# A two-layer hybrid decoder on one core: a temporary in another buffer, the removal rate ahead of the receptance, and recurrence and query steps that follow no weight split

## The chip, the cores and the metric

One core of a Trainium2 chip runs the whole kernel in one launch. The metric is the device time of one execution in microseconds. In the profile PE is TensorE (matmuls), PEld its weight loads, DVE is VectorE, ACT is ScalarE, POOL is GpSimd, and SP is SyncE, which here only issues transfers. All data are float32.

## The reference, cut to what matters

Two layers on `x` of 1 x 256 x 2048. Each layer makes one wide input projection, feeds three mixers with its column groups, and ends in an output projection with a layer norm:

```python
for l in range(DEPTH):                       # 2 layers
    u = x @ w_in[l]
    (cb, cc, ch, cg, cq, ckv, kpe, mg, rcols, rg) = _split(u, IN_SIZES)
    y_conv = _short_conv_branch(cb, cc, ch, cg, conv_w[l])                # 512 columns
    y_mla = _mla_branch(cq, ckv, kpe, mg, ..., w_uq[l], w_ukv[l], cos, sin)  # 8 heads, 1024 columns
    y_rwkv = _rwkv7_branch(rcols, rg, ...)                                # 8 heads x 64
    mix = jnp.concatenate([y_conv, y_mla, y_rwkv], axis=-1)
    x = _layer_norm(DEEPNORM_ALPHA * x + mix @ w_out[l], ln_g[l], ln_b[l])
```

The RWKV mixer takes from `rcols` a receptance r, a key k, a value v, a decay w and a removal rate a (the last two by small two-step projections, `tanh(wd) @ w2` and `ad @ a2`), and runs this recurrence over the 256 positions:

```python
def step(state, inp):
    r_t, w_t, k_t, v_t, a_t, b_t = inp       # a = -kk, b = kk * a
    sa = jnp.einsum('bhvk,bhk->bhv', state, a_t)
    state = (state * w_t[:, :, None, :] + sa[..., None] * b_t[:, :, None, :]
             + v_t[..., None] * k_t[:, :, None, :])
    return state, jnp.einsum('bhvk,bhk->bhv', state, r_t)
```

## The kernel before

**Projections.** The input projection of a layer is cut into groups of 512 columns, named by what they give: `k`, `r`, `a` (removal rate and decay inputs with the attention's key and value inputs), `v`, `cq`, the convolution's `cc`, `ch`, `cb`, `cg`, and the gates `rg`, `mg0`, `mg1`. The list `MAIN` sets the order of the first ten. Then come the attention's second projections `ukv` and `uq`, then `mg0` and `mg1`, then the output projection `po`. A product is made from split operands: each float32 factor is a high part plus a low part, and `mm3` issues three matmuls for one (lines L338, L339, L340: high x high, high x low, low x high). A group is 16 row blocks of the weight x 4 column blocks x 3 = 192 matmuls, each 128x128 against 128x256.

**Weights.** SP loads a group's weight in four pieces of 1 MB (tiles `w_<group>`, three buffers). Each piece is split twice: ACT casts the high part (`hi_<group>`), DVE subtracts it for the low part (`lo_<group>`). There are four buffers of each, and one buffer pair feeds 24 matmuls.

**The mixers.** The branch code is written as generators (`rwkv`, `latent` for the attention, `conv`). For every weight split that PE consumes, `tick()` advances each running generator to its next `yield`; `until(name)` lets a generator wait until a group's matmuls are issued. A scheduler lays out every engine's order ahead of time by a simulated time line; steps issued under `tc.high_priority(AHEAD)` or `(EVICT)` go ahead of others. Each engine then runs its own list in that order, with semaphores where one waits for another.

**The gate.** `V` and `A` wrap VectorE and ScalarE. With `GATE = 'V'`, every VectorE step issued through `V` inside a tick is ordered behind the weight split two ahead of the one in use (`OFF = 2`). It is an order only, no semaphore. A step issued with `nc.vector` directly has no such bond, and `gates.clear()` takes it from the rest of a tick. `A` carries none in this setting.

**RWKV, step by step.** `rwkv_k` takes the key (`kx`, and its norm by `ksq`, `rn`, `kkn`). `rwkv_r` takes the receptance (`rx`). `rwkv_decay` mixes the decay and removal inputs (`wax`), splits them (`wah` on ACT, `wal` on DVE) and projects them with the split weight `was` in 16 matmuls (`pw`, `pa`; L528 and L529), then `sig`, `cum` and `pe`. `rwkv_products` makes the chunk products (`pg`, `gs`, from `ar` and `bk`), and SP carries them through DRAM in eight transfers `bd<-gs`. `rwkv_inverse` solves a triangular system by 31 steps on DVE, each with the temporary `tm` in pool `sm`, which has two buffers for a tag. `rwkv_pairs` transposes the keys and others (`pk`, L709). `rwkv_chain` is the recurrence over four chunks of 64 positions: PE `prh` (L782), DVE `rhs`, PE `pu` (L789), DVE and ACT `uvt`, PE `pst`, DVE `st`, which is the next chunk's state; after every second chunk PE makes the outputs `py` (L758, L767). `rwkv_norm` and `rwkv_gate` (`th_rg`) follow. These matmuls are small and use a half of the array's rows.

**Attention.** `mla_kv` makes keys and values (`pkn`, `pvt`), `mla_q` the queries (`pqn`, `pqp`), and `mla_attend` splits queries (`split_queries` into tiles `qk`, and `q1`) and runs the softmax over the heads.

PSUM has two pools of four buffers each: one for the accumulators of groups, one for everything else.

Of the kernel before, what the change touches and what calls it, by code (L numbers as in the profile page):

```python
# [10 lines left out]
F32 = mybir.dt.float32  # L11
# [3 lines left out]
ALU = mybir.AluOpType  # L15
AX = mybir.AxisListType

P = 128
D = 2048
S = 256  # L20
# [4 lines left out]
AHEAD = 1500  # L25
EVICT = 4000
# [84 lines left out]
def hybrid_layers(ctx: ExitStack, tc: tile.TileContext, x, positions, xT, w_in, w_out, w_uq, w_ukv, par, wa_in, gb_in,  # L111
                  gbp, cst, eye32, sums, out):
    nc = tc.nc
# [8 lines left out]
    sm = ctx.enter_context(tc.tile_pool(name="sm", bufs=2))  # L122
    dr = ctx.enter_context(tc.tile_pool(name="dr", bufs=1, space=bass.MemoryType.DRAM))

    gates, splits = {}, []
# [18 lines left out]
    V, A, G, T = Gated(nc.vector, "V"), Gated(nc.scalar, "A"), nc.gpsimd, nc.tensor  # L144
# [151 lines left out]
    def until(name):  # L296
        while name not in done:
            yield
# [46 lines left out]
        for i, src in enumerate((hi, lo)):  # L345
            T.matmul(o, ones[:, which * P:which * P + P], src, start=i == 0, stop=i == 1)

    MAIN, LATE, ORDER = ("k", "r", "a", "v", "cq", "cc", "ch", "cb", "cg", "rg"), ("mg0", "mg1"), (0, 12, 4, 8)

    def plan():  # L350

# [84 lines left out]
    def rwkv(l, pq, u, t):  # L436
        yield from until(f"k{l}")
        yield from rwkv_k(l, pq, t, u["k"][0])
        yield from until(f"r{l}")
        yield from rwkv_r(l, pq, t, u["r"][0])  # L440
        yield from until(f"a{l}")
        yield from rwkv_decay(l, pq, t, u["a"][0][0])
        yield from rwkv_scale(l, pq, t)
        yield from rwkv_products(l, t)
        inv = rwkv_inverse(l, t)
        while f"v{l}" not in done:
            next(inv)
            yield
        yield from rwkv_v(l, pq, t, u["v"][0])
        fill = rwkv_pairs(l, t)  # L450
        while True:
            a, b = next(inv, "end"), next(fill, "end")
            if a == b == "end":
                break
            yield
        yield from rwkv_chain(l, t)
        done.add(f"chain{l}")
        yield from rwkv_norm(l, pq, t)
        yield from until(f"heads{l}")
        yield from rwkv_gate(l, t)  # L460
# [166 lines left out]
    def rwkv_inverse(l, st):  # L627
        gs = st["gs"]
        bd = dr.tile([64, 32, 32], F32, tag=f"bd{l}", name=f"bd{l}")
        for par in range(2):  # L630
            for k in range(2):
                r = slice(par * 64 + k * 32, par * 64 + k * 32 + 32)
                u0 = (par * 2 + k) * 16
                for i in range(2):
                    src = gs[i].rearrange("p c (b q) t -> p c b q t", q=2)[r, :, :, par, k * 32:k * 32 + 32]
                    nc.sync.dma_start(bd[u0 + 8 * i:u0 + 8 * i + 8].rearrange("(c b) i j -> i c b j", b=4), src)
        bt = s4(f"bt{l}", (64, 32, 32))
        nc.sync.dma_start(bt, bd)
        xi = s4(f"xi{l}", (64, 32, 32))
        after(nc.sync.dma_start(xi, eye32.rearrange("p (i j) -> p i j", j=32)), st["mark"])  # L640
        yield
        yield
        yield
        n = 0
        for j in range(31, 0, -1):
            w = 32 - j
            tm = sm.tile([64, j, w], F32, tag="rt", name=f"tm{l}_{j}")
            V.tensor_tensor(tm, bt[:, 0:j, j:j + 1].to_broadcast([64, j, w]),
                            xi[:, j:j + 1, j:32].to_broadcast([64, j, w]), ALU.mult)
            V.tensor_tensor(xi[:, 0:j, j:32], xi[:, 0:j, j:32], tm, ALU.add)  # L650
            n += 1
            if n == 3:
                yield
                n = 0
        xd = dr.tile([64, 32, 32], F32, tag=f"xd{l}", name=f"xd{l}")
        nc.sync.dma_start(xd, xi)
        xq = s4(f"xq{l}", (P, 4, 4, 64))
        xt1 = sm.tile([P, 4, 4, 32], F32, tag="s", name=f"xt1{l}")
        V.memset(xq, 0.0)
        yield  # L660
        for par in range(2):
            for k in range(2):
                r = slice(par * 64 + k * 32, par * 64 + k * 32 + 32)
                u0 = (par * 2 + k) * 16
                nc.sync.dma_start(xq[r, :, :, k * 32:k * 32 + 32],
                                    xd[u0:u0 + 16].rearrange("(c b) i j -> i c b j", b=4))
        yield
        yield
        for par in range(2):
            r = slice(par * 64, par * 64 + 32)  # L670
            t1 = V.transpose(xt1[r].rearrange("p c b t -> p (c b) t"), xq[r, :, :, 0:32].rearrange("p c b t -> p (c b) t"))
        yield
        zs = sm.tile([P, 16, 32], F32, tag="s", name=f"zs{l}")
        quarters = [(slice(par * 64, par * 64 + 32), slice(par * 64 + 32, par * 64 + 64)) for par in range(2)]
        pz = [pm.tile([P, 16, 32], F32, tag="m", name=f"pz{l}_{par}") for par in range(2)]
        for c in range(4):
            for b in range(4):
                for par, (ra, rb) in enumerate(quarters):
                    m = T.matmul(pz[par][rb, c * 4 + b, :], gs[c // 2][ra, c % 2, 2 * b + par, 32:64],
                                 xt1[ra, c, b, :], start=True, stop=True)  # L680
                    if c == b == par == 0:
                        gather(m, [t1])
        for par, (ra, rb) in enumerate(quarters):
            z1 = V.tensor_copy(zs[rb], pz[par][rb])
        yield
        px = [pm.tile([P, 16, 32], F32, tag="m", name=f"px{l}_{par}") for par in range(2)]
        for c in range(4):
            for b in range(4):
                for par, (ra, rb) in enumerate(quarters):
                    m = T.matmul(px[par][ra, c * 4 + b, :], zs[rb, c * 4 + b, :], xq[rb, c, b, 32:64],  # L690
                                 start=True, stop=True)
                    if c == b == par == 0:
                        gather(m, [z1])
        for par, (ra, rb) in enumerate(quarters):
            st["xq1"] = V.tensor_copy(xq[ra, :, :, 32:64].rearrange("p c b t -> p (c b) t"), px[par][ra])
        yield
        st["xq"] = xq
# [47 lines left out]
    def rwkv_chain(l, st):  # L745
# [28 lines left out]
        for c in range(4):  # L774
            cc = slice(c * 64, (c + 1) * 64)
            if state is None:
                rhs = qs[:, 0]
            else:
                pr_ = pm.tile([P, 4, 64], F32, tag="m", name=f"prh{l}_{c}")
                for b in range(4):  # L780
                    for par in range(2):
                        T.matmul(pr_[rs[par], b, :], ar[rs[par], b, 0, cc], state[rs[par], b, :], start=True, stop=True)  # L782
                rhs = slot("rhs", f"rhs{l}_{c}", (P, 4, 64), 2)
                V.tensor_tensor(rhs, pr_, qs[:, c], ALU.add)
                yield
            pu = pm.tile([P, 4, 64], F32, tag="m", name=f"pu{l}_{c}")
            for b in range(4):
                for par in (1, 0):
# [3 lines left out]
            moved = []  # L792
            for par in range(2):
                dst = uvt[:, c].rearrange("p (b q) t -> p b q t", q=2)[rs[par], :, par, :]
                if par == 0:
                    moved.append(V.tensor_copy(dst, pu[rs[par]]))
                else:
                    moved.append(A.copy(dst, pu[rs[par]]))
            yield
            if c < 3:  # L800
                pst = pm.tile([P, 4, 64], F32, tag="m", name=f"pst{l}_{c}")
                for b in range(4):
                    for par in (1, 0):
                        h = 2 * b + par
                        m = T.matmul(pst[rs[par], b, :], bkt[:, c, h, :], uvt[:, c, h, :], start=True, stop=True)
                        if b == 0 and par:
                            gather(m, moved)
                new = slot("st", f"st{l}_{c}", (P, 4, 64), 2)
                pc_ = pe[:, c::4, 64:65].to_broadcast([P, 4, 64])
                if state is None:  # L810
                    V.tensor_tensor(new, pst, pc_, ALU.mult)
                else:
                    V.tensor_tensor(new, pst, state, ALU.add)
                    V.tensor_tensor(new, new, pc_, ALU.mult)
            before.append(state)
            if c % 2:
                out(c // 2, before[-2:], moved)
# [199 lines left out]
    def mla_attend(l, st):  # L1017
# [4 lines left out]
        def split_queries(h):  # L1022
            t = qk[h % 2]
            split_in(t[:, 0, 0:P], t[:, 1, 0:P], qn[:, h, P:S])
# [3 lines left out]
            split_queries(h)  # L1028
            split_keys(st, h)

        split_queries(0)
        for par in range(2):
            r, o = halves[par], halves[1 - par]
            of = lambda rr: q1.rearrange("p (g q) t -> p q g t", q=2)[rr, par]
            A.copy(of(r), qp[r, :, P:S])
            V.tensor_tensor(of(o), qp[r, :, P:S], of(r).bitcast(F32), ALU.subtract)
        split_queries(1)
        yield
        live = {}
        both = ((0, slice(0, 128)), (1, slice(128, 384)))  # L1040

# [362 lines left out]
```

## Time and profile before

| what | value |
|---|---|
| median of three runs | 920.2 us (920.05 to 921.54) |
| profiled execution, own time | 919.2 us |
| its span | 917.4 us |
| instructions | 18371 |
| mean granted TensorE clock | 0.996 of full speed |
| ACT busy | 467.1 us, 51% |
| POOL busy | 22.2 us, 2% |
| moved by DMA | 165.12 MB, mean 180 GB/s |

The span is what the hardware profiler saw of one execution; that execution's own time has 1.8 us around it. A profile row of a timeline gives the start in us, the duration in us, the engine, the line, the operation, output<-inputs with buffer numbers left out, sizes, and in brackets the idle time just before and what ended it. A helper records most steps of DVE and ACT, so these all carry line L137 and are told apart by tile names. The ends of matmuls are modelled; their starts are what to compare.

### The profile page before, as it was taken

Reading aid. Unit: us, or ns where it says so; the run is one execution under the profiler, and the core shown is the slowest. Engines: PE = TensorE matmul, PEld = TensorE weight load, DVE = VectorE, ACT = ScalarE, POOL = GpSimd, SP = SyncE. Lnnn points to the kernel's source line nnn. Section 1 sums busy time; section 2 is a strip of 40 time slices with the busy share of each in tenths; the row PEclk is TensorE's granted clock in tenths of the full one; section 3 lists DMA queues with packets and bytes.
Section 4 is the critical chain, followed back from the end, with each engine's and each line's share of the span. In section 5 each row is a group of like instructions: output and inputs, shape, how many; then the busy total and the mean of one; then the engine's idle time right before and its main releaser. Section 6 shows DMA issues by size and latency. Waiting matters only on the chain.

```text
span 917.4 us, 18371 instructions
## 1 busy us (share of the span) xinstructions
PE 905.3 (99%) x7719; PEld 865.5 (94%) x7719; DVE 670.8 (73%) x1122; ACT 467.1 (51%) x716; POOL 22.2 (2%) x47
## 2 busy tenths in 40 slices
PE   8999999999999999999999999999999999999996
PEld 8999999999999999888899999999999999998895
DVE  6686887885659986666766679878855599866665
ACT  6756546343447576434246474563424566764430
POOL 1210000000000000000010000000000000000000
PEclk9999999999999999999999999999999999999998
DMA  8955463455343643955565545545552456259442
GB/s 312 295 187 184 139 202 134 161 185 177 123 150 128 229 139 124 362 205 162 201 212 184 184 149 185 162 139 185 186 160 93 151 172 216 107 178 348 172 131 91
DMA packets 47523, 165.12 MB, mean 180 GB/s; under 512 B 13446, under 2 KB 22198, under 8 KB 32582
## 3 DMA queue, kind: packets, MB, share of 16 engines
q1 hardware_dynamic: 39680, 150.35, 47.9%
q10 hardware_dynamic: 5072, 9.57, 3.2%
q0 software_dynamic: 2688, 4.03, 1.6%
q8 instruction: 60, 0.98, 0.4%
q14 instruction: 23, 0.19, 0.1%
HBM read 158.61 MB, written 5.32 MB: 179 GB/s over the span
## 4 chain that ended last, share of the span: by engine, by line
PE 95%; DVE 2%; DMA 2%; ACT 0%; SPq 0%; issue 0%; DVEq 0%; ACTq 0%
PE po L338 6%; PE po L340 6%; PE po L339 6%; PE u_mg L340 3%; PE u_mg L338 3%; PE u_mg L339 3%; PE u_cc L338 2%; PE u_cg L340 2%; PE u_rg L340 2%; PE u_cq L340 2%; PE u_rg L338 2%; PE u_cg L338 2%; PE u_cb L340 2%; PE u_cb L339 2%; PE u_cb L338 2%; PE u_ch L339 2%
## 5 line engine op out<-in xcount | busy, mean ns | idle before, releaser
L137 DVE TENSOR_TENSOR lo_wo<-w_wo,hi_wo 128x1024 fp32r<-128x1024 f32 x57 | 69.3, 1222 | 45.9 <-ACT hi_wo L137 44.5
L137 ACT CAST hi_wo<-w_wo 128x1024 fp32r<-128x1024 f32 x57 | 59.7, 1052 | 72.9 <-PE po L340 61.5
L339 PE MATMUL u_mg<-x,hi_mg 128*128 128x256 f32 x256 | 72.7, 284 | 0.0
L340 PE MATMUL u_mg<-x,lo_mg 128*128 128x256 f32 x256 | 72.5, 283 | 0.0
L338 PE MATMUL u_mg<-x,hi_mg 128*128 128x256 f32 x256 | 72.1, 283 | 0.0
L340 PEld LDWEIGHTS u_mg<-x,lo_mg 128*128 128x128 f32 x256 | 49.1, 192 | 0.0
L339 PEld LDWEIGHTS u_mg<-x,hi_mg 128*128 128x128 f32 x256 | 49.0, 192 | 0.0
L338 PEld LDWEIGHTS u_mg<-x,hi_mg 128*128 128x128 f32 x256 | 48.9, 192 | 0.0
L339 PE MATMUL po<-lo_wo,ma 128*128 128x512 f32 (+1 forms) x128 | 46.4, 362 | 0.0
L340 PE MATMUL po<-hi_wo,ma 128*128 128x512 f32 (+1 forms) x128 | 46.4, 362 | 0.0
L338 PE MATMUL po<-hi_wo,ma 128*128 128x512 f32 (+1 forms) x128 | 45.9, 363 | 0.0
L137 DVE TENSOR_TENSOR lo_mg<-w_mg,hi_mg 128x1024 fp32r<-128x1024 f32 x32 | 38.9, 1221 | 7.2 <-ACT hi_mg L137 7.0
L137 ACT CAST hi_mg<-w_mg 128x1024 fp32r<-128x1024 f32 x32 | 33.5, 1048 | 17.0 <-PE u_mg L339 11.4
L338 PE MATMUL u_cc<-x,hi_cc 128*128 128x256 f32 x128 | 37.2, 290 | 0.0
L340 PE MATMUL u_cg<-x,lo_cg 128*128 128x256 f32 x128 | 37.0, 289 | 0.0
L340 PE MATMUL u_rg<-x,lo_rg 128*128 128x256 f32 x128 | 37.0, 289 | 0.0
L338 PE MATMUL u_rg<-x,hi_rg 128*128 128x256 f32 x128 | 36.8, 288 | 0.0
L338 PE MATMUL u_k<-x,hi_k 128*128 128x256 f32 x128 | 36.2, 287 | 0.4 <-ACT hi_k L137 0.4
L338 PE MATMUL u_cg<-x,hi_cg 128*128 128x256 f32 x128 | 36.4, 284 | 0.0
L339 PE MATMUL u_k<-x,hi_k 128*128 128x256 f32 x128 | 36.2, 286 | 0.0
L338 PE MATMUL u_a<-x,hi_a 128*128 128x256 f32 x128 | 36.2, 283 | 0.0
L339 PE MATMUL u_a<-x,hi_a 128*128 128x256 f32 x128 | 36.2, 283 | 0.0
(421 smaller groups left out, 3375.7 us busy)
## 6 DMA issues: line engine op xcount, KB each, us to landing
w_wo<-in_w_out_dram SPq DMA_DIRECT2D x24, 1024.0 KB, 5.2
w_mg<-in_w_in_dram SPq DMA_DIRECT2D x16, 1024.0 KB, 4.8
w_r<-in_w_in_dram SPq DMA_DIRECT2D x8, 1024.0 KB, 6.1
w_a<-in_w_in_dram SPq DMA_DIRECT2D x8, 1024.0 KB, 4.8
w_v<-in_w_in_dram SPq DMA_DIRECT2D x8, 1024.0 KB, 4.9
w_cq<-in_w_in_dram SPq DMA_DIRECT2D x8, 1024.0 KB, 4.9
w_cc<-in_w_in_dram SPq DMA_DIRECT2D x8, 1024.0 KB, 4.9
w_ch<-in_w_in_dram SPq DMA_DIRECT2D x8, 1024.0 KB, 4.9
```

The costliest lines, as they stand in the source:

```text
L137: inst = call(*args, **kwargs)
L338: m = T.matmul(o, lh, rh, start=first, stop=False, skip_group_check=True)
L339: T.matmul(o, lh, rl, start=False, stop=False, skip_group_check=True)
L340: T.matmul(o, ll, rh, start=False, stop=last, skip_group_check=True)
```

## The change

Four edits. (1) The inverse's temporary `tm` takes its buffers from tag "s" of the same pool instead of tag "rt". (2) Group `a` is projected ahead of group `r`, and `rwkv` runs the decay ahead of the receptance. (3) In the recurrence `rhs`, `uvt` and `st` on VectorE are issued with `nc.vector` under `high_priority(EVICT)`, so that the gate does not hold them, and the `yield` after `rhs` is gone. (4) `mla_attend` clears the gate and issues the query splits and `q1` at high priority, in another order, without a `yield` behind them.

```diff
-    MAIN, LATE, ORDER = ("k", "r", "a", "v", "cq", "cc", "ch", "cb", "cg", "rg"), ("mg0", "mg1"), (0, 12, 4, 8)
+    MAIN, LATE, ORDER = ("k", "a", "r", "v", "cq", "cc", "ch", "cb", "cg", "rg"), ("mg0", "mg1"), (0, 12, 4, 8)
...
         yield from rwkv_k(l, pq, t, u["k"][0])
+        yield from until(f"a{l}")
+        yield from rwkv_decay(l, pq, t, u["a"][0][0])
         yield from until(f"r{l}")
         yield from rwkv_r(l, pq, t, u["r"][0])
-        yield from until(f"a{l}")
-        yield from rwkv_decay(l, pq, t, u["a"][0][0])
...
-            tm = sm.tile([64, j, w], F32, tag="rt", name=f"tm{l}_{j}")
+            tm = sm.tile([64, j, w], F32, tag="s", name=f"tm{l}_{j}")
...
-                V.tensor_tensor(rhs, pr_, qs[:, c], ALU.add)
-                yield
+                with tc.high_priority(EVICT):
+                    nc.vector.tensor_tensor(rhs, pr_, qs[:, c], ALU.add)
...
-                if par == 0:
-                    moved.append(V.tensor_copy(dst, pu[rs[par]]))
-                else:
-                    moved.append(A.copy(dst, pu[rs[par]]))
+                with tc.high_priority(EVICT):
+                    moved.append((A.copy if par else nc.vector.tensor_copy)(dst, pu[rs[par]]))
...
-                if state is None:
-                    V.tensor_tensor(new, pst, pc_, ALU.mult)
-                else:
-                    V.tensor_tensor(new, pst, state, ALU.add)
-                    V.tensor_tensor(new, new, pc_, ALU.mult)
+                with tc.high_priority(EVICT):
+                    if state is None:
+                        nc.vector.tensor_tensor(new, pst, pc_, ALU.mult)
+                    else:
+                        nc.vector.tensor_tensor(new, pst, state, ALU.add)
+                        nc.vector.tensor_tensor(new, new, pc_, ALU.mult)
...
-        split_queries(0)
-        for par in range(2):
-            r, o = halves[par], halves[1 - par]
-            of = lambda rr: q1.rearrange("p (g q) t -> p q g t", q=2)[rr, par]
-            A.copy(of(r), qp[r, :, P:S])
-            V.tensor_tensor(of(o), qp[r, :, P:S], of(r).bitcast(F32), ALU.subtract)
-        split_queries(1)
-        yield
+        gates.clear()
+        with tc.high_priority(AHEAD):
+            for par in range(2):
+                r, o = halves[par], halves[1 - par]
+                of = lambda rr: q1.rearrange("p (g q) t -> p q g t", q=2)[rr, par]
+                A.copy(of(r), qp[r, :, P:S])
+                V.tensor_tensor(of(o), qp[r, :, P:S], of(r).bitcast(F32), ALU.subtract)
+                split_queries(par)
```

How the instructions stand shows at three places. In these rows a number behind a name tells its pieces and copies apart, and differs from one kernel to the other. First, VectorE's list around the decay's copies `wal` in layer 0, where `lo_v` and `lo_r` are weight splits of the groups then running. Before:

```order
L137 TENSOR_TENSOR was_936<-wa_935,was_936 64x512 x2
L137 TENSOR_TENSOR lo_v_4_0_980<-w_v_4_977,hi_v_4_0_979 128x1024
L137 SCALAR_TENSOR_TENSOR wax_945<-u_a_0_697,pars,wax_945 128x255
L137 TENSOR_TENSOR kpe_961<-u_a_0_697,cosT 128x256
L137 TENSOR_TENSOR rt_k_962<-u_a_0_697,sinT 32x256 x4
L137 TENSOR_TENSOR lo_v_4_2_984<-w_v_4_977,hi_v_4_2_983 128x1024
L137 TENSOR_TENSOR kpe_961<-kpe_961,rt_k_962 128x256
L137 TENSOR_TENSOR wal_942<-wax_945,wah_954 64x256 x2
L137 TENSOR_TENSOR sumkv_973<-skv_0_970 128x256
L137 TENSOR_TENSOR lo_v_8_0_1070<-w_v_8_1067,hi_v_8_0_1069 128x1024
```

The same place on VectorE after:

```order
L137 TENSOR_TENSOR lo_r_4_0_737<-w_r_4_734,hi_r_4_0_736 128x1024
L137 SCALAR_TENSOR_TENSOR ksq_408<-ksq_408,rn_628 128x1024
L137 SCALAR_TENSOR_TENSOR wax_702<-u_a_0_428,pars,wax_702 128x255
L137 TENSOR_TENSOR kpe_718<-u_a_0_428,cosT 128x256
L137 TENSOR_TENSOR rt_k_719<-u_a_0_428,sinT 32x256 x4
L137 TENSOR_TENSOR lo_r_4_2_741<-w_r_4_734,hi_r_4_2_740 128x1024
L137 SCALAR_TENSOR_TENSOR rn_628<-ksq_408,rn_628 128x1024
L137 TENSOR_TENSOR wal_699<-wax_702,wah_711 64x256
L137 TENSOR_TENSOR kpe_718<-kpe_718,rt_k_719 128x256
L137 TENSOR_TENSOR lo_r_8_0_827<-w_r_8_824,hi_r_8_0_826 128x1024
L137 TENSOR_TENSOR wal_699<-wax_702,wah_711 64x256
```

The copies now stand among the splits of group r and the key norm's last steps (`ksq`, `rn`), and a split comes between the two `wal`.

Second, TensorE's list around the first `pk` transposes of layer 0. Before:

```order
L340 MATMUL u_cc_1_1587<-x_0_82,lo_cc_0_2_1507 128x256
L709 MATMUL pk_0_0_1678<-cs,bk_1197 128x64 x8
L709 MATMUL pk_0_1_1689<-cs,bk_1197 128x64 x8
L338 MATMUL u_cc_0_1586<-x_1_83,hi_cc_4_0_1590 128x256
L339 MATMUL u_cc_0_1586<-x_1_83,hi_cc_4_0_1590 128x256
```

TensorE after, at the same transposes:

```order
L340 MATMUL u_cq_1_1297<-x_3_85,lo_cq_12_2_1458 128x256
L709 MATMUL pk_0_0_1594<-cs,bk_1115 128x64 x8
L709 MATMUL pk_0_1_1605<-cs,bk_1115 128x64 x8
L709 MATMUL pk_1_0_1616<-cs,bk_1115 128x64 x8
L709 MATMUL pk_1_1_1627<-cs,bk_1115 128x64 x8
L338 MATMUL u_cc_0_1648<-x_0_82,hi_cc_0_0_1520 128x256
```

The four sets of `pk` stood in two blocks with matmuls of cc between; now they stand together, at the end of group cq.

Third, VectorE's list at the start of the recurrence of layer 0. Before:

```order
L137 COPY uvt_1785<-pu_0_2527 64x4x64
L137 TENSOR_TENSOR lo_rg_0_0_3045<-w_rg_0_3042,hi_rg_0_0_3044 128x1024
L137 TENSOR_TENSOR lo_rg_0_2_3049<-w_rg_0_3042,hi_rg_0_2_3048 128x1024
L137 TENSOR_TENSOR st_0_2571<-pst_0_2562,pe_1127 128x256
L137 TENSOR_TENSOR lo_rg_4_0_3127<-w_rg_4_3124,hi_rg_4_0_3126 128x1024
L137 TENSOR_TENSOR rhs_1_2616<-prh_1_2607,qs_1924 128x256
```

VectorE there after:

```order
L796 COPY uvt_1684<-pu_0_2418 64x4x64
L137 TENSOR_TENSOR lo_cg_12_0_3005<-w_cg_12_3002,hi_cg_12_0_3004 128x1024
L810 TENSOR_TENSOR st_0_2476<-pst_0_2467,pe_884 128x256
L137 TENSOR_TENSOR lo_cg_12_2_3009<-w_cg_12_3002,hi_cg_12_2_3008 128x1024
L785 TENSOR_TENSOR rhs_1_2518<-prh_1_2509,qs_1820 128x256
L137 TENSOR_TENSOR lo_rg_0_0_3063<-w_rg_0_3060,hi_rg_0_0_3062 128x1024
```

From `uvt` to `rhs` there are two weight splits between, where there were three, and they belong to cg and no longer to rg.

## The prediction

> **What bounds the kernel now.** I read the head of the page first (busy times and the chain by engine), then PE's waits, then two windows with idle in them, then the timelines of PE, ACT and DVE at the places that the change moves.
>
> ```profile
> span 917.4 us, 18371 instructions
> PE 905.3 (99%) x7719; PEld 865.5 (94%) x7719; DVE 670.8 (73%) x1122; ACT 467.1 (51%) x716; POOL 22.2 (2%) x47
> PE 95%; DVE 2%; DMA 2%; ACT 0%; SPq 0%; issue 0%; DVEq 0%; ACTq 0%
> ```
>
> PE is busy for 905.3 of 917.4 us and makes up 95% of the chain that ended last. DVE (73%) and ACT (51%) cannot set the end by their sums; they can only make PE wait. All of PE's waits (total, times, longest):
>
> ```profile
> PE cwt L1225 <- DVE cw L137: 2.3, 2, 1.4
> PE pzero L243 <- DVE zeror L137: 2.0, 1, 2.0
> PE xt L1246 <- PE pz L1278: 0.9, 1, 0.9
> PE u_k L340 <- DVE lo_k L137: 0.5, 1, 0.5
> PE u_k L338 <- ACT hi_k L137: 0.4, 1, 0.4
> PE lw L1234 <- DVE ct L137: 0.4, 1, 0.4
> ```
>
> They come to 6.5 us: `pzero` and `u_k` at the start, the others in the layer norm, at the layer boundary and at the end. Not one names a tile of the decay, the recurrence, the inverse or the queries. The windows at the boundary and the end say the same (length, busy time of PE, PEld, DVE, ACT, POOL, then the granted clock, DMA share, GB/s):
>
> ```profile
> 440.00:460.00 20.00, 18.13 (x129) 15.84 (x127) 15.27 (x40) 6.13 (x10) 0.73 (x1) 1.00 0.46 170
> 900.00:917.00 17.00, 10.14 (x59) 8.08 (x57) 9.50 (x24) 0.29 (x1) 0.00 (x0) 0.81 0.37 123
> ```
>
> PE's idle there is 20.00 − 18.13 = 1.87 and 17.00 − 10.14 = 6.86 us. With the 2.0 + 0.5 + 0.4 = 2.9 us of waits at the start that is 11.6 of the 917.4 − 905.3 = 12.1 us that it idles at all. Nothing is left to win in the middle by feeding PE earlier. What is left is PE's own pace, and two small things in it:
>
> ```profile
> 138.46 0.28 PE L340 MATMUL u_cc<-x,lo_cc 128*128 128x256 f32 x1
> 138.67 1.01 PE L709 MATMUL pk<-cs,bk 64*128 64x64 f32 x16
> 139.61 0.39 PE L338 MATMUL u_cc<-x,hi_cc 128*128 128x256 f32 x1
> 139.84 0.28 PE L339 MATMUL u_cc<-x,hi_cc 128*128 128x256 f32 x1
> 139.96 0.28 PE L340 MATMUL u_cc<-x,lo_cc 128*128 128x256 f32 x1
> ...
> 142.67 1.02 PE L709 MATMUL pk<-cs,bk 64*128 64x64 f32 x16
> ```
>
> The starts are what to read, since the ends are modelled. A full matmul follows the last one after 0.12 us (139.84 to 139.96). Into a block of 64-row matmuls it is 0.21 us (138.46 to 138.67), and out of it 0.23 (139.61 to 139.84). Entering and leaving one costs (0.21 − 0.12) + (0.23 − 0.12) = 0.20 us, whatever the block holds.
>
> **The change, part by part.**
>
> *The temporary's other buffer.* `tm` goes from tag "rt" to "s". No instruction is added. If the new tag made the inverse wait for a reader, DVE would pause and nobody on PE would notice before a weight split came late; if it frees a wait, DVE ends earlier into idle time. Both are nought while the splits keep their lead, which the decay's and queries' parts below put at 1.8 to 8 us.
>
> *Group a and the decay ahead of r.* The 192 matmuls of either group stay. The decay's 16 matmuls and its copies on ACT and DVE now stand in group r, and the receptance's steps in group v. Here each operand must still be ready when PE comes to it, and PE comes in program order:
>
> ```profile
> 54.33 0.48 ACT L137 ACTIVATE rx<-u_r,pc 128x256 f32<-128x256 f32 x1 [0.86 <-PE u_r L340]
> 77.31 0.47 ACT L137 ACTIVATE wax<-u_a,pc 128x256 f32<-128x256 f32 x1 [1.23 <-PE u_a L340]
> 77.91 1.05 ACT L137 CAST hi_v<-w_v 128x1024 fp32r<-128x1024 f32 x1
> 82.98 0.41 ACT L137 CAST wah<-wax 64x256 fp32r<-64x256 f32 x1
> 77.83 0.28 PE L338 MATMUL u_v<-x,hi_v 128*128 128x256 f32 x1
> 84.07 0.28 PE L528 MATMUL pw<-wah,was 128*128 128x256 f32 x1
> 508.67 0.47 ACT L137 ACTIVATE rx<-u_r,pc 128x256 f32<-128x256 f32 x1 [1.18 <-PE u_r L340]
> ```
>
> Before, ACT takes up `u_a` at 77.31, the last `wah` is done at 82.98 + 0.41 = 83.39, that is 6.08 us on, and PE's `pw` stands at 84.07, 6.76 us on: 0.7 us of lead. After, `u_a` is ready where `u_r` was, 54.33. By the order ACT has one more weight cast between (1.05 us): last `wah` at 54.33 + 6.08 + 1.05 = 61.5. `pw` stands 67 matmuls into r where it stood 52 into v: 54.33 + 6.76 + 15 × 0.12 = 62.9. Lead 1.4 us. In layer 1 no cast comes between and `pw` stands 56 in: 508.67 + 6.08 = 514.8 against 508.67 + 6.76 + 0.5 = 515.9, lead 1.1.
>
> The low halves come by DVE, whose row after is known in order, so I lay the measured lengths on it:
>
> ```profile
> 37.79 1.04 ACT L137 CAST was<-wa 128x1024 fp32r<-128x1024 f32 x1
> 53.83 1.23 DVE L137 SCALAR_TENSOR_TENSOR ksq<-ksq,rn 128x1024 f32<-128x1024 f32 x1
> 54.98 1.22 DVE L137 TENSOR_TENSOR lo_a<-w_a,hi_a 128x1024 fp32r<-128x1024 f32 x1
> 78.22 0.41 DVE L137 TENSOR_TENSOR kpe<-u_a,cosT 128x256 f32<-128x256 f32 x1
> 78.65 1.72 DVE L137 TENSOR_TENSOR rt_k<-u_a,sinT 32x256 f32<-32x256 f32 x4
> 82.06 0.87 DVE L137 TENSOR_TENSOR wal<-wax,wah 64x256 fp32r<-64x256 f32 x2
> ```
>
> The decay's own weights `wa` are no limit: their transfers keep their place in POOL's row, and ACT already reads them at 37.79. A wide step starts 1.15 us after the last (53.83 to 54.98). From 53.83: `lo_r_4_0`, `ksq` (two wide steps) to 56.1, `wax` and `kpe` 0.4 each to 56.9, `rt_k` 1.75 to 58.7, `lo_r_4_2`, `rn` to 61.0, first `wal` 0.45, `kpe` 0.4 to 61.8, `lo_r_8_0` to 63.0, second `wal` to 63.4. Its first reader on PE stands 7 matmuls of r and 4 of `pw`/`pa` after 62.9: 64.2. Lead 0.8 us, the smallest that the change makes. So the term is 0. If the cover is gone PE waits by as much as the copy is late: a lead of 0.8 lost to one more wide step (1.15) costs 0.4 us, to two 1.5. Below nothing it cannot go, since PE does not wait there now.
>
> With the products earlier, six of their eight DMAs (`bd<-gs`) pass the load of `w_cc_4` in SP's queue, and all eight that of `w_cc_8`, and hold them while they wait for `gs`:
>
> ```profile
> 109.53 7.47 SPq L385 DMA_DIRECT2D w_cc<-in_w_in_dram  x3
> 120.17 8.36 SPq L636 DMA_DIRECT2D bd<-gs  x8
> ```
>
> Before, the eight took until 128.5. After, the first product stands 92 rows earlier on PE, about 11 us, so they are through at about 117.5 and the two loads go out then instead of at 109.5 to 117.0: at most 8 us late. PE comes to `w_cc_4` at 139.61 (the `u_cc` row behind `pk` above), so 22 us are left for a transfer and two splits. Term 0.
>
> *The recurrence's steps ungated.* `rhs`, `uvt` and `st` go on DVE as soon as they can, and no longer behind the weight split of the tick. Nothing is added on PE. On DVE each is queued ahead of one or two splits, which then stand behind its wait:
>
> ```profile
> 229.32 1.23 DVE L137 TENSOR_TENSOR lo_rg<-w_rg,hi_rg 128x1024 fp32r<-128x1024 f32 x1 [1.09 <-ACT hi_rg L137]
> 264.20 0.42 DVE L137 TENSOR_TENSOR rhs<-prh,qs 128x256 f32<-128x256 f32 x1 [0.55 <-PE prh L782]
> 268.46 0.28 PE L340 MATMUL u_rg<-x,lo_rg 128*128 128x256 f32 x1
> 270.95 0.68 DVE L137 SCALAR_TENSOR_TENSOR th_rg<-th_rg,u_rg 128x512 f32<-128x512 f32 x1
> 274.07 0.28 PE L338 MATMUL pvt<-hi_ukv,hkv 128*128 128x256 f32 x1
> 236.16 0.28 PE L338 MATMUL u_cg<-x,hi_cg 128*128 128x256 f32 x1
> ```
>
> `lo_rg` is done at 230.55, and at 236.16 PE is still in cg, a group earlier: more than 5 us of lead. A wait such as `rhs`'s 0.55 us, or that and two wide steps of 1.15, is 0.6 to 2.9 us and fits. Since the recurrence runs earlier, the last `py` block no longer stands among the `pkn`/`pvt` matmuls. The second `pvt` group needs the PSUM buffer that the gate frees at 270.95 + 0.68 = 271.63; it stood at 274.07, and now 36 matmuls after the end of rg: 268.46 + 37 × 0.12 = 272.9. Lead 2.4 becomes 1.3. Term 0.
>
> *Queries.* The steps of `split_queries` and `q1` come at once and ahead, and fewer DVE steps stand before the last split of uq, which has the smallest weight lead in the trace:
>
> ```profile
> 296.49 0.95 DVE L137 TENSOR_TENSOR lo_uq<-w_uq,hi_uq 128x768 fp32r<-128x768 f32 x1
> 299.27 0.36 PE L340 MATMUL pqn<-hq,lo_uq 128*128 128x256 f32 x1
> ```
>
> It is done at 297.44 and read at 299.27, so it has 1.8 us. After, one short step instead of eleven stands between it and the split before, and ahead of the first mg split there are four steps instead of two (about 1.3 us more). Term 0 again: a lead that grows pays nothing.
>
> *PE's own order.* The same matmuls. The two `pk` blocks of a layer, 4 us apart above, become one: 0.20 us a layer, 0.4 in all. The blocks of the recurrence stay as many (13 a layer). Against this the moved blocks split other triples of matmuls; summing the spacings that the trace shows for each pair of neighbours over both orders gave −0.1 us. Taken −0.3, bounds −0.4 and 0.
>
> **Sum.** The profiled execution took 919.2 us (span 917.4 and 1.8 around it), 1.0 below the median of the runs, 920.2. 919.2 − 0.3 + 0 = 918.9 on its clock; with the 1.0 back, 919.9, called 920.0: no change. 0.2% or 1.84 us is about what a measurement of this kernel can tell from none.
>
> **The rivals.**
>
> *Slower: a copy or a buffer late at PE's new place.* The decay has leads of 0.8 to 1.4 us, `pvt` 1.3. DVE's chain above is laid end to end; two more wide steps ahead of `wal`, or a split of r that waits for a buffer, would turn 0.8 into a wait. From then each us of lateness is a us. One wide step late at three places in both layers: 6 × 0.4 = 2.4 us → 922.3; two at one place a layer: 2 × 1.5 = 3 → 923. For it: the lead before was only 0.7 at `pw`, and PE did not wait. Against: the order itself stretches the place by 15 matmuls. 12 in 100.
>
> *Slower: the ungated steps hold the splits back.* PE starves if `rhs`, `uvt` or `st` waits on DVE for longer than the splits' lead. At 5 us of lead this needs four or more wide steps behind a wait of a block; 2 us at one place a layer would give 924. Against: `rhs` waits 0.55. 5 in 100. The Trainium skill speaks for this rival ("Perfetto Trace Analysis", section Tensor Engine Instruction): ACT and DVE are strictly first in, first out, while PE may pull weight loads ahead, so an early step that waits holds all behind it. By that rule the split behind `rhs` is late by `rhs`'s whole wait; the 0.55 us of the row is that, and less than the lead, so by the rule too the sum stays.
>
> *Faster: the boundary.* If DVE, relieved earlier, reached the layer norm's steps sooner, up to 1.87 us at the boundary and the 1.4 of `cwt` at the end could go: 920.0 − 3.3 = 916.7 at most, half of it 918.2. Against: from the first splits of the output projection on, the rows of PE, ACT and DVE are the same in both orders, and what DVE does there hangs on PE's last sums. 8 in 100.
>
> *The change does nothing at all*, the scheduler having kept the steps where they were, would be 920.2. The orders show that it moves them; it is inside the forecast.
>
> **How the numbers follow.** No change holds 75 in 100, its own range 919 to 921.5 (the three runs spread 1.5 us). The two slower rivals together have 17, the faster one 8. To hold 8 in 10, the range takes the forecast and the near half of each side: 918.3 (a layer boundary's worth gained) to 922.9 (the copies one or two steps late). Chances: faster 0.08, same 0.75, slower 0.17.
>
> **What would show it.** In PE's waits no `pw`, `pa`, `pvt`, `u_rg` or `pqn` appears, or each under 0.3 us; PE's busy time is 905 within 0.5; one `pk` block a layer of 32; `cwt` waits 2.3 again; `rhs` and `uvt` wait on DVE as now, with splits after them. A `pw <- wah` or `pa <- wal` of 0.4 us or more, or a `u_r` that waits for `lo_r`, is the first rival; `u_cg` or `u_rg` waiting for a split the second; a smaller idle in the window at the boundary the third. I am wrong if PE's pace itself changes, with no wait shown, by more than 0.5 us.

## The result, and the profile after

The changed kernel takes 916.05 us (median of four runs, 915.27 to 916.55) against 920.87 us for the kernel before in the same session. The ratio is 0.9947, with a 95% interval of 0.9930 to 0.9964: 4.8 us faster, where no change was forecast and 918.3 was the low end of the range. The profiled execution took 915.89 us, its span 914.1.

The head of the page after:

```profile
span 914.1 us, 18358 instructions
PE 901.8 (99%) x7719; PEld 862.2 (94%) x7719; DVE 666.5 (73%) x1122; ACT 466.8 (51%) x716; POOL 24.1 (3%) x47
```

PE runs the same 7719 instructions, and is busy for 901.8 us where it was 905.3. So 3.5 us have gone out of PE's own work and not out of its waits. PE's waits after (total, times, longest) say which of them changed:

```profile
PE pzero L243 <- DVE zeror L137: 2.0, 1, 2.0
PE cwt L1224 <- DVE cw L137: 1.4, 1, 1.4
PE u_k L338 <- ACT hi_k L137: 1.4, 1, 1.4
PE xt L1245 <- PE pz L1277: 0.9, 1, 0.9
PE u_k L340 <- DVE lo_k L137: 0.5, 1, 0.5
PE lw L1233 <- DVE ct L137: 0.4, 1, 0.4
```

No tile of the decay, the recurrence or the queries appears, as before. Two rows moved: `cwt` lost its wait of 0.9 us at the layer boundary, and the first `hi_k` cost 1.0 more at the start, where the changed kernel has the same instructions. These two cancel here.

The work that shrank is the small half-row matmuls. First the products `pg` of layer 0, before, each block with the full matmul that follows it (start, duration, and x passes; a float32 matmul such as `pg` is recorded as two passes, a transpose such as `pk` as one):

```profile
115.31 1.16 PE L609 MATMUL pg<-ar,bk 64*128 64x128 f32 x8
116.39 0.39 PE L340 MATMUL u_cq<-x,lo_cq 128*128 128x256 f32 x1
...
116.94 2.05 PE L609 MATMUL pg<-ar,bk 64*128 64x128 f32 x24
118.92 0.39 PE L340 MATMUL u_cq<-x,lo_cq 128*128 128x256 f32 x1
...
122.35 2.38 PE L609 MATMUL pg<-ar,bk 64*128 64x128 f32 x32
124.66 0.38 PE L340 MATMUL u_cq<-x,lo_cq 128*128 128x256 f32 x1
```

and after:

```profile
105.89 2.06 PE L609 MATMUL pg<-ar,bk 64*128 64x128 f32 x32
107.88 0.39 PE L338 MATMUL u_cq<-x,hi_cq 128*128 128x256 f32 x1
...
109.74 1.49 PE L609 MATMUL pg<-ar,bk 64*128 64x128 f32 x16
111.16 0.38 PE L340 MATMUL u_cq<-x,lo_cq 128*128 128x256 f32 x1
...
113.98 1.16 PE L609 MATMUL pg<-ar,bk 64*128 64x128 f32 x16
115.08 0.39 PE L338 MATMUL u_cq<-x,hi_cq 128*128 128x256 f32 x1
```

Compare the first block before with the last one after: 8 passes take 1.08 us (115.31 to 116.39), and 16 passes of the same shape take 1.10 (113.98 to 115.08). The order says what differs. The last figure ahead of a name's running number is the half: `pg_0_1` uses rows 64 to 127 of the array, `pg_0_0` rows 0 to 63. Before, at the first block and the start of the second:

```
L609 MATMUL pg_0_1_1333<-ar_1198,bk_1197 128x128 x4
...
L609 MATMUL pg_0_0_1332<-ar_1198,bk_1197 128x128 x4
```

and the first of the same matmuls after:

```
L609 MATMUL pg_0_1_1273<-ar_1116,bk_1115 128x128
L609 MATMUL pg_0_0_1272<-ar_1116,bk_1115 128x128
L609 MATMUL pg_0_1_1273<-ar_1116,bk_1115 128x128
L609 MATMUL pg_0_0_1272<-ar_1116,bk_1115 128x128
```

Four of one half in a row run one after the other; one of each half in turn run side by side. Single passes in the two traces say it more sharply: in a run of one half they start 0.11 us apart; in turn, two start within 0.01 us of each other and the next two 0.11 us later. The middle block after lies between: its order has three of one half, three of the other and then one of each, and its 16 passes take 1.42 us (109.74 to 111.16). The inverse's `pz` shows it too; it uses 32 rows, out of one half or the other. Its order begins with fourteen of one half and fourteen of the other before, and with six and six after:

```profile
216.65 1.98 PE L679 MATMUL pz<-xt,gs 32*32 32x32 f32 x64
218.56 0.38 PE L340 MATMUL u_cg<-x,lo_cg 128*128 128x256 f32 x1
```

```profile
209.58 1.47 PE L679 MATMUL pz<-xt,gs 32*32 32x32 f32 x64
210.98 0.38 PE L339 MATMUL u_cb<-x,hi_cb 128*128 128x256 f32 x1
```

The transposes `pk` still stand in runs of eight of one half, as before, but in one block:

```profile
133.45 1.63 PE L709 MATMUL pk<-cs,bk 64*128 64x64 f32 x32
135.01 0.39 PE L338 MATMUL u_cc<-x,hi_cc 128*128 128x256 f32 x1
```

The sum for a layer, by starts: `pg` 1.08 + 1.98 + 2.31 = 5.37 becomes 1.99 + 1.42 + 1.10 = 4.51, so 0.86 less; `pz` 1.91 becomes 1.40, 0.51 less; `pk` 0.94 + 0.95 becomes 1.56, 0.33 less, and one entry and exit of 0.20 is saved. That is 1.90 a layer and 3.8 us in two (PE does the same in layer 1). The spans of the two profiled executions differ by 3.3 and the medians by 4.8, so the blocks give the bulk of the gain, but not its last microsecond. Layer 1 alone is a cleaner measure, since neither the start nor the wait at the boundary is in it: it runs from the first `cwt` at the boundary to the first one of the last norm. Before and after:

```profile
448.98 0.27 PE L1225 MATMUL cwt<-cs,cw 128*5 128x128 f32 x1 [0.89 <-DVE cw L137]
900.16 0.27 PE L1225 MATMUL cwt<-cs,cw 128*5 128x128 f32 x1
```

```profile
447.66 0.27 PE L1224 MATMUL cwt<-cs,cw 128*5 128x128 f32 x1
896.96 0.27 PE L1224 MATMUL cwt<-cs,cw 128*5 128x128 f32 x1
```

That is 451.18 us before and 449.30 after, 1.88 less, where the blocks say 1.90.

### The profile page after: what moved, and what is told of

Read it like the earlier page. It is cut to its first block, busy times and chain, and to the rows that moved or that the text cites. A ratio compares the mean times of both kernels' runs of the same rounds, so it can differ in the third digit from the quotient of the medians.

```text
span 914.1 us, 18358 instructions
## 1 busy us (share of the span) xinstructions
PE 901.8 (99%) x7719; PEld 862.2 (94%) x7719; DVE 666.5 (73%) x1122; ACT 466.8 (51%) x716; POOL 24.1 (3%) x47
## 4 chain that ended last, share of the span: by engine, by line
PE 93%; DMA 4%; DVE 1%; ACT 0%; issue 0%; SPq 0%; POOL 0%; DVEq 0%; ACTq 0%
PE po L338 6%; PE po L340 6%; PE po L339 6%; PE u_mg L338 3%; PE u_mg L339 3%; PE u_mg L340 3%; PE u_rg L340 2%; PE u_cc L338 2%; PE u_cg L339 2%; DMA xt<-in_xT_dram 2%; PE u_cq L338 2%; PE u_cg L338 2%; PE u_cb L339 2%; PE u_rg L338 2%; PE u_cg L340 2%; PE u_cq L340 2%
## 5 line engine op out<-in xcount | busy, mean ns | idle before, releaser
L339 PE MATMUL u_cg<-x,hi_cg 128*128 128x256 f32 x128 | 36.8, 288 | 0.0
L338 PE MATMUL u_cq<-x,hi_cq 128*128 128x256 f32 x128 | 36.6, 286 | 0.0
L338 PE MATMUL u_cg<-x,hi_cg 128*128 128x256 f32 x128 | 36.6, 286 | 0.0
L339 PE MATMUL u_cb<-x,hi_cb 128*128 128x256 f32 x128 | 36.4, 285 | 0.0
```

What stands on the lines that cost most here:

```text
L338: m = T.matmul(o, lh, rh, start=first, stop=False, skip_group_check=True)
L339: T.matmul(o, lh, rl, start=False, stop=False, skip_group_check=True)
```

## The experiments

Two theories were put against each other. *Row halves*: the change reorders small matmuls so that more of them overlap. *Relief of VectorE*: the steps taken off the gate free VectorE ahead of the layer boundary. A third, small one: *fewer blocks*. Each row compares medians of two kernels on one chip:

| run | us, median | before | ratio (95%) | pg, layer 0 | pz, layer 0 | wait at the boundary | layer 1 |
|---|---|---|---|---|---|---|---|
| e1, order alone | 915.90 | 920.49 | 0.9949 (0.9934 to 0.9964) | 4.51 | 1.40 | 1.06 | 449.37 |
| e2, the other three edits | 921.60 | 920.49 | 1.0008 (0.9996 to 1.0020) | 5.37 | 2.45 | 1.29 | 451.20 |
| e3, before, alternated | 916.47 | 920.49 | 0.9949 (0.9933 to 0.9965) | 4.29 | 1.13 | 1.05 | 449.13 |
| e4, after, in runs | 919.67 | 920.49 | 0.9985 (0.9976 to 0.9994) | 5.60 | 2.04 | 0.50 | 450.97 |
| e5, after again | 915.37 | 920.01 | 0.9950 (0.9938 to 0.9963) | 4.51 | 1.40 | 0 | 449.32 |
| e6, after, alternated | 914.50 | 920.01 | 0.9940 (0.9928 to 0.9953) | 4.51 | 1.13 | 0 | 448.51 |
| e7, e6 with blocks merged | 912.98 | 920.01 | 0.9928 (0.9915 to 0.9942) | 4.51 | 1.13 | 0 | 447.84 |
| e8, edits 2 and 4 | 916.81 | 920.29 | 0.9964 (0.9949 to 0.9979) | 4.51 | 1.40 | 1.09 | 449.38 |
| e9, edits 1, 2 and 3 | 917.69 | 920.29 | 0.9968 (0.9955 to 0.9981) | 4.51 | 1.40 | 0 | 449.32 |

The `pg` and `pz` columns are the us from a block's start to the next full matmul, as above, for all blocks. The wait is the time ahead of the first `cwt` over the usual 0.12 us of spacing (1.05 before). The last column is layer 1 as measured above (451.18 before).

**Which edit.** e1 is edit 2 alone, the reordered `MAIN` and `rwkv` of the diff:

> The kernel before with edit 2 alone (group a and the decay ahead of r); the temporary, the recurrence's steps and the query splits as before. Row-half theory (two f32 matmuls of 64 or 32 rows that lie in different halves of the array run side by side, two in the same half do not; the order of pg and pz alternates the halves more often after the change): the gain is whole, -3.3 to -4.8 us, pg 10.7 to about 9.0 us and pz 11.1 to 10.1 on PE. Rival, relief of VectorE (the ungated steps free it ahead of the layer boundary): at most -0.5 us, since nothing is ungated here. Rival, fewer blocks (each entry into the half-row mode costs 0.2 us): -0.4 us.

The 11.1 us of `pz` in it must count a tile of the same name in the layer norm too, since the inverse's two blocks take 2 × 1.91 us.

e2 is the other three edits on the kernel before:

> The kernel before with edits 1, 3 and 4 (temporary's buffer, ungated recurrence steps, ungated query splits), but with r ahead of a as before. Row-half theory: pg, pz and pk stand as before in the same order, so 0 within 0.5 us. Relief of VectorE: -1 to -4.8 us, and the wait at the layer boundary is gone. Fewer blocks: 0, as there are 44 as before.

The gain is in the order, 4.6 us by e1, and none in the rest: e2 is 1.1 us slower by the medians, more than the 0.5 that was allowed, with an interval that holds no change. Layer 1 says the same more sharply, 1.8 us less in e1 and 0.0 in e2. One block of e2 did change: in layer 0 `pz` comes 4 us earlier than before and waits in its middle for `xt` from VectorE, so it holds 2.45 us (1.91 in layer 1):

```profile
212.57 1.07 PE L679 MATMUL pz<-xt,gs 32*32 32x32 f32 x28
213.90 1.19 PE L679 MATMUL pz<-xt,gs 32*32 32x32 f32 x36 [0.26 <-DVE xt L137]
215.02 0.38 PE L338 MATMUL u_cg<-x,hi_cg 128*128 128x256 f32 x1
```

Which of edits 1, 3 and 4 brings `pz` ahead of its operand was not tested.

**Is it the halves?** e3 takes the kernel before, with none of the edits, and binds the order of `pg` (and of `pz` and `px` likewise) without a semaphore:

```diff
-                for par in (1, 0):
+                for par in (0, 1) if c < 2 else (1, 0):
                     ...
-                    if b == 0 and par:
+                    if b == 0 and par == (c > 1):
                         gather(m, st["ready"][c])
+                    elif c != 2:
+                        after(m, last)
+                    last = m
```

> The kernel before; none of the four edits. Only the order of pg, pz and px on TensorE is fixed by order bonds without a semaphore, so that the halves alternate: pg in 2 blocks a layer (16 and 16 matmuls) instead of 3, pz and px one after the other. VectorE's work, the weight splits and the groups stay. Row-half theory: pg 5.4 to 4.3 us a layer, pz 1.9 to 1.1, px 1.2 to 1.1, 2.0 a layer, -4 us in all. Relief of VectorE: 0. Fewer blocks: one block less a layer, -0.4 us.

Its `pg` and `pz` in layer 0:

```profile
119.01 2.06 PE L609 MATMUL pg<-ar,bk 64*128 64x128 f32 x32
120.99 0.39 PE L339 MATMUL u_cq<-x,hi_cq 128*128 128x256 f32 x1
...
123.46 2.38 PE L609 MATMUL pg<-ar,bk 64*128 64x128 f32 x32
125.77 0.38 PE L340 MATMUL u_cq<-x,lo_cq 128*128 128x256 f32 x1
...
219.45 1.20 PE L682 MATMUL pz<-xt,gs 32*32 32x32 f32 x64
220.58 0.38 PE L339 MATMUL u_cg<-x,hi_cg 128*128 128x256 f32 x1
```

`pg` 1.98 + 2.31 = 4.29 us, `pz` 1.13: 1.08 and 0.78 less than before. With `px` (1.21 to 1.13) and one block less it is 2.14 a layer, 4.3 in two, and layer 1 shows 2.05. The median fell by 4.0 us, as expected, without any of the four edits. The scheduler moved other steps a little too (the first `pk` stands at 139.78 where it stood at 138.67), but the groups stand in the old order, the wait at the boundary is still 1.05, and PE's waits name no new tile. e4 goes the other way, from the changed kernel, whose blocks it keeps:

```diff
-            for b in range(4):
-                for par in (1, 0):
+            turns = [(b, par) for b in range(4) for par in (1, 0)]
+            if c % 2:
+                turns.sort(key=lambda t: -t[1])
+            for b, par in turns:
...
-        for c in range(4):
-            for b in range(4):
-                for par, (ra, rb) in enumerate(quarters):
+        for par, (ra, rb) in enumerate(quarters):
+            for c in range(4):
+                for b in range(4):
...
```

> The changed kernel with all four edits and the same 42 blocks; only the order inside some blocks is turned: pg of chunks 1 and 3 does four matmuls of one half and then four of the other, and pz sixteen and sixteen. Row-half theory: pg +0.85 us for each of the two chunks and pz +0.65, 2.35 a layer, 4.7 us slower than the changed kernel, so the kernel before within about 1.5 us. Relief of VectorE and fewer blocks: as fast as the changed kernel, -3.3 to -4.8 us against before.

```profile
106.35 2.60 PE L611 MATMUL pg<-ar,bk 64*128 64x128 f32 x32
108.89 0.39 PE L338 MATMUL u_cq<-x,hi_cq 128*128 128x256 f32 x1
...
114.99 1.71 PE L611 MATMUL pg<-ar,bk 64*128 64x128 f32 x16
116.63 0.39 PE L338 MATMUL u_cq<-x,hi_cq 128*128 128x256 f32 x1
...
211.13 2.11 PE L684 MATMUL pz<-xt,gs 32*32 32x32 f32 x64
213.17 0.38 PE L339 MATMUL u_cb<-x,hi_cb 128*128 128x256 f32 x1
```

The blocks are the changed kernel's 42, but the first holds 2.54 us instead of 1.99, the last 1.64 instead of 1.10, `pz` 2.04 instead of 1.40: 1.73 a layer, 3.5 in all (4.7 were expected: I had put 0.85 on each of the two chunks of `pg`, and it was 0.55). Layer 1 is 1.67 us longer than after. Of the 4.8 us the median keeps 0.8; the wait at the boundary, of which 0.50 came back here, has a part in that. So the order of the halves gives the gain and takes most of it away, with all four edits in place.

**How far it goes.** e5 is the changed kernel once more; e6 alternates `pz`, `px` and `pk` throughout, e7 also joins `pv`'s and `pq`'s two blocks (the `yield` stands behind the loop, no longer in it):

> The changed kernel itself, on the same chip as the next two. Row-half theory: 4 to 5 us faster than before; pg 9.5, pz 3.0, pk 3.3 us on PE. On the wait at the layer boundary: if its loss in the profile of the changed kernel (1.04 us before, none after) is the change's doing, it is none here too; if it is the landing of the load of w_k that differs from run to run, it is anything from 0 to 1.3 us.

> The changed kernel with its same 42 blocks; pz, px and the transposes pk fixed so that the halves alternate throughout (pg stays as it is but for its order bonds). Row-half theory: pz 1.40 to 1.1 us a layer, px 1.21 to 1.1, pk 1.56 to 1.05, 0.9 a layer, 1.8 us faster than the changed kernel. If the order of the halves were used up: the same as the changed kernel.

> The kernel of the run before this one, and pv's two blocks of a layer made one, and pq's two, by one yield instead of two (38 blocks instead of 42). Each merged block saves the 0.20 us of entering and leaving the half-row mode: 4 x 0.2 = 0.8 us faster than the run before this one, 2.6 faster than the changed kernel. If a block's entry cost nothing, or if the longer block made PE wait for its operands, the same as or slower than the run before this one.

For e6, `pk` and `pz` in layer 0:

```profile
133.31 1.22 PE L716 MATMUL pk<-cs,bk 64*128 64x64 f32 x32
134.46 0.39 PE L338 MATMUL u_cc<-x,hi_cc 128*128 128x256 f32 x1
...
209.74 1.20 PE L682 MATMUL pz<-xt,gs 32*32 32x32 f32 x64
210.87 0.38 PE L339 MATMUL u_cg<-x,hi_cg 128*128 128x256 f32 x1
```

`pk` 1.56 to 1.15, `pz` 1.40 to 1.13, `px` 1.21 to 1.13: 0.76 a layer, 1.5 us. The medians differ by 0.9 (915.37 to 914.50) and the spans by 1.0 (913.3 to 912.3); the two intervals of the ratio overlap, so the medians alone don't show it. The blocks do, and so does layer 1, which is 0.81 us shorter than in e5. For e7, `pv` is one block where e6 has two:

```profile
138.24 1.15 PE L731 MATMUL pv<-cs,vx 64*64 64x64 f32 x32
139.31 0.38 PE L346 MATMUL prskv<-shkv,ones 128*128 128x256 f32 x1
```

The second takes 1.08 us (141.88 to 142.96). In e7:

```profile
137.80 2.08 PE L731 MATMUL pv<-cs,vx 64*64 64x64 f32 x64
139.81 0.38 PE L346 MATMUL prskv<-shkv,ones 128*128 128x256 f32 x1
```

1.07 + 1.08 becomes 2.01, and an entry and an exit of 0.20 fall away: 0.34 a merge, more than the 0.20 that I had. The rest stands at the ends of a block: in e7's `pv` pairs of passes follow each other by 0.06 us, but the second pair follows the first by 0.11 and the full matmul stands 0.15 us behind the last pass. Four merges make 1.4 us. The median of e7 is 1.5 below e6, though the intervals overlap; layer 1, with two of the merges, is 0.67 shorter. At 912.98 us e7 is the fastest of all: 2.4 us below the changed kernel, 7.0 below the one before.

**The wait at the boundary.** In the changed kernel ACT gets the first piece of the next layer's `w_k` earlier. Before and after:

```profile
442.53 2.00 ACT L137 CAST hi_k<-w_k 128x1024 fp32r<-128x1024 f32 x2 [4.60 <-DMA w_k<-in_w_in_dram]
```

```profile
439.88 2.00 ACT L137 CAST hi_k<-w_k 128x1024 fp32r<-128x1024 f32 x2 [2.52 <-DMA w_k<-in_w_in_dram]
```

In e1 the same cast starts at 442.57. DVE's `lo_k` waits for `hi_k`, and the norm's steps that lead to `cw` and `cwt` stand behind `lo_k` in its list. Two kernels ask which edits bring the load in:

> Edits 2 and 4 alone (order, query splits). Row-half theory: pg 9.5, pz 3.0 and pk 3.3 us on PE as in the changed kernel, the whole gain but for the layer boundary. On the wait at the boundary, which was 1.04 us before, 1.06 with edit 2 alone, 1.29 with edits 1, 3 and 4, and none in the profiles with all four: none if edits 2 and 4 together take it away, about 1.0 if the recurrence's edits are needed.

> Edits 1, 2 and 3 (temporary, order, recurrence), without the query edit. Row-half theory: pg 9.5, pz 3.0, pk 3.3 us on PE. Wait at the boundary: none if the recurrence's edits with the order take it away, about 1.0 us if the query edit is needed.

With edits 2 and 4 the wait is 1.09, with 1, 2 and 3 it is gone, and e2, without edit 2, has 1.29. That points to the order together with the recurrence's steps (or the temporary). It is not shown: each figure is from one profiled execution, and e4, with all four edits, still has 0.50. Why the load lands sooner is open too: SP begins to issue the four loads of `w_k` no earlier (435.12 us after, 434.77 before), and I did not find what they share the transfer with. Nor do the medians confirm it: e1, with the wait, has 0.9949 and e9, without it, 0.9968, which overlap. It is a microsecond seen in the profiles alone. The same medians set a limit on what they can tell: e1, e8 and e9 have the same half-row blocks and layer 1 within 0.06 us, and yet gain 4.6, 3.5 and 2.6 us. Where these 2 us come from was not found.

## Why the prediction was wrong

- **The step that failed** is the last term of the sum, "PE's own order": "summing the spacings that the trace shows for each pair of neighbours over both orders gave −0.1 us. Taken −0.3, bounds −0.4 and 0". I took one mean spacing for a `pg` that follows a `pg`. That mean hid two prices. By the blocks it is some 0.13 us a pass in a run of one half (1.08 us for 8 passes, entry lag included) and 0.07 where the halves alternate (1.10 for 16). The term was −3.8 us by the blocks, 1.88 in layer 1 alone; the blocks were in the trace before, and the orders, which list `x4` against single rows, were before me. The prediction named this sign itself: it is wrong if PE's pace changes, with no wait shown, by more than 0.5 us. It was 3.5. The Trainium skill says ("TensorEngine Tiling (Array Packing)", section Key Properties) that different tiles of the array can execute in parallel. The trace agrees: 16 passes in turn take 1.10 us, 8 of one half 1.08. No rival of the prediction weighed that.
- **"Nothing is left to win in the middle by feeding PE earlier"** was right as it stands and misled me. A PE that is busy at 99% can still be busy with work laid out badly, and its busy time fell by 3.5 us with the same instructions.
- **`pk` merged**: forecast 0.40 for both layers, measured 2 × 0.53 = 1.06, because the merged block is itself shorter than the two (1.89 to 1.56 us a layer). Right in direction, small by a factor of 2.6. The order inside, runs of eight, is the same. Two things fit and were not separated: the ends of a block cost more than the 0.20 (e7), and the merged block has three places where the half changes instead of two, at each of which the trace has some passes of the two halves side by side.
- **The decay's leads** held. Its second `wal` and its reader on PE, after:

```profile
64.69 0.41 DVE L137 TENSOR_TENSOR wal<-wax,wah 64x256 fp32r<-64x256 f32 x1
65.76 0.40 PE L529 MATMUL pa<-wal,was 128*128 128x256 f32 x2
```

  The copy is done at 65.10, so the lead is 0.66 us where 0.8 was worked out. No PE wait names `wal`, `pvt` or `pqn`, so the slower rivals fell. The terms of 0 for the temporary, the recurrence and the queries fit too: edits 1, 3 and 4 together show no change beyond the interval (e2).
- **The faster rival, the boundary,** was named at its place, with 1.87 us at most. In the profile after, the first `cwt` has lost its 0.9 us. What came earlier there is the landing of `w_k`; that a relieved VectorE brings it, as this rival had it, is not shown. And e1 and e3 gain their 4.0 to 4.6 us with that wait still there, so it is chance that the measured time lies near this rival's 916.7.

## What to carry to other kernels

Where matmuls use half of the array or less, count them by the part that they use and look in the order at which part follows which: alternate them, and bind the order, since alternating in the source is not enough: the source of `pg` takes the halves in turn in both kernels, and the scheduler still issued runs of four before and of three after. What made it do so was not tested. Before a spacing is used as a price, split it by everything that can differ between two neighbours; a mean over one name mixed two prices that differ by a factor of two. And a bound engine at 99% is a reason to read its blocks one by one, not a reason to expect nothing.

## What the runs showed of the hardware

- Float32 matmuls of 64 rows by 128 columns against 64x128, two passes each, take 1.10 us for 16 passes in alternation (after), 1.42 with runs of three (after) and 1.64 in two runs of four (e4). For 32 passes it is 1.98 us in alternation (e3) and 2.31 to 2.54 where parts of the block stand in runs (before and e4). The 32-row `pz` takes 1.13 us for 64 passes when it alternates throughout, and 2.04 in two runs.
- Joining two half-row blocks of `pv` is worth 0.34 us and not only the 0.20 of entry and exit (e7).
